# Hybrid SSD and attention layer on one core: the two parts of q and of k in one DRAM tile and one load per head pair

## The chip, the cores and the metric

The kernel runs on one core of one Trainium2 chip. The metric is the device time of one execution in microseconds (us). Three timed runs of the kernel before gave 1282.12, 1282.40 and 1283.06 us, a median of 1282.4 us. One further execution was recorded by the hardware profiler; all rows quoted in this document are of such recorded executions.

## The reference

One decoder layer over 1024 tokens of width 1024, all in float32. A normalised input goes through one wide projection, whose columns feed two branches; the branches are gated, merged, projected once more and added to the input:

```
h    = rmsnorm(x, pre_g)
proj = h @ w_in              # -> z_ssm, xBC, dt, q, k, v, f, z_att, g_ssm, g_att
y    = ssd(silu(conv(xBC)), dt, ...)  -> * silu(z_ssm) -> group rmsnorm     # Mamba-2 branch
F    = cumsum(log_sigmoid(f + fgate_b))
for each block of 128 queries, 16 heads of 64:
    s = (q . k) / 8 + F[query] - F[key], causal
    o = softmax(s) @ v
y_att  = o * silu(z_att)
merged = sigmoid(g_ssm) * (y @ w_branch_ssm) + sigmoid(g_att) * (y_att @ w_branch_att)
x + rmsnorm(merged @ w_out, post_g)
```

What the change touches is `q . k`: the scores of the attention branch.

## The kernel before, in words

**Arithmetic.** A float32 product is made from matmuls with rounded operands ("fp32r"): each operand is split into a rounded high part and the rest, the low part, and a product is the sum of three matmuls: high by high, high by low, low by high. The large matrix products (projection, branches, output) run on blocks of 512 with a scheme of seven block products in place of eight. The classes and helpers for it make a stream of steps: a weight block `raw` (256 KB) is loaded from DRAM (L344, SyncE's queue), sums of blocks are formed by VectorE (L357), ScalarE rounds the high part (L351), VectorE takes the rest (L352), TensorE multiplies into PSUM banks `pb`, `pc`, `pd` (recorded at L130, where every matmul has its line), and ScalarE and VectorE empty the banks into `s` (L404) and `th`, `u` (L412 to L418). The operands named `x0h`, `x0l` to `x6h`, `x6l` are the high and low parts of the input blocks; they are loaded (L265) and split (L280, L281) ahead of their step.

**Stages.** Until about 660 us the kernel computes the projection and, woven into it, the Mamba-2 branch. From about 665 to 1120 us it runs attention, head pair by head pair, while the stream of block products goes on beside it (first the remaining projections, `za`, the gates `gs` and `ga`, then the branch products). From 1120 us to the end come the merge, the output projection and the last norm.

**q and k.** After their projection, q and k come out transposed: channels on the 128 partitions (two heads of 64 make one head pair, of which there are 8, `NK`), tokens along the row. `parts` (L642) handles each half of the tokens (`ch`): ScalarE writes the scaled, rounded high part into a tile `hi` (L652), VectorE the rest in place (L653), and the two are stored to two DRAM tiles, the high one through ScalarE's DMA queue (L654) and the low one through SyncE's queue SP (L655). The DRAM tiles are `qh_dram`, `ql_dram`, `kh_dram`, `kl_dram`, each [8 head pairs, 128 partitions, 1024 tokens].

**Attention.** A head pair has six groups of query blocks:

```
GROUPS = [((7, 6), 1), ((7, 6), 0), ((5, 4), 1), ((5, 4), 0), ((3, 2), 0), ((1, 0), 0)]
```

The first entry is a pair of query blocks, the second is the half of the keys. For these groups the loads are issued ahead, by `loads(m)` (L1587): `load_q` (L1322) brings 256 query columns of the high and of the low part into one tile `q` [128, 2, 256], which has two buffers, with two DMAs of 128 KB, `load_k` (L1329) brings 512 key columns of both parts into one tile `k` [128, 2, 512], with one buffer for each half of the keys, with two DMAs of 256 KB, and then the forget-gate bias `fb` [128, 2, 512], broadcast to all partitions, with a third of 512 KB (L1335). `scores` makes three pairs of matmuls from q and k into the bank `s`, VectorE adds the bias and takes the row extreme `nm` (L1474), ScalarE takes the exponential `ex` (L1478), TensorE transposes it (`pt`, L133, the line of every transpose), and ScalarE or VectorE copy it out as `p` (L1515, L1517) for the product with v (`av`).

**What sets the order.** The Python code of attention yields after each piece of work, and an interleaver gives the stream of block products its turns beside it, so the order in which instructions stand in each engine's queue comes from modelled costs and from the order of the program. Each engine then works through its own queue strictly in order, and waits on semaphores. SP issues nearly all loads (x, `raw`, q, k, `fb`, x0 to x6, `y`) and some stores (`za_dram`, the low parts); ScalarE issues stores too, among them the gates `gs_dram` and `ga_dram` (L622) and the high parts (L654). The tiles `th` come from one pool with four buffers.

Of the kernel before, what the change touches and what calls it, by code (L numbers as in the profile page):

```python
# [8 lines left out]
F32 = mybir.dt.float32  # L9
# [7 lines left out]
P = 128  # L17
T = 1024
D = 1024
NK = D // P  # L20
# [66 lines left out]
def hybrid_layer(ctx: ExitStack, tc, a, out):  # L87

    nc = tc.nc
# [25 lines left out]
    za_dram = tc.dram_tile([NK, P, T], F32, name="za_dram")  # L115
    gs_dram = tc.dram_tile([NK, P, T], F32, name="gs_dram")
    ga_dram = tc.dram_tile([NK, P, T], F32, name="ga_dram")
    qh_dram = tc.dram_tile([NK, P, T], F32, name="qh_dram")
    ql_dram = tc.dram_tile([NK, P, T], F32, name="ql_dram")
    kh_dram = tc.dram_tile([NK, P, T], F32, name="kh_dram")  # L120
    kl_dram = tc.dram_tile([NK, P, T], F32, name="kl_dram")
    v_dram = tc.dram_tile([NK, P, NT, P], F32, name="v_dram")
    ys_dram = tc.dram_tile([NK, P, T], F32, name="ys_dram")
    ya_dram = tc.dram_tile([NK, P, T], F32, name="ya_dram")
# [13 lines left out]
    def small(name="th"):  # L138
        return gp.tile([P, HALF], F32, tag="th", name=name)
# [21 lines left out]
    class Operands:  # L161
# [127 lines left out]
        def put(self, j, **parts):  # L289
            for name, raw in parts.items():  # L290
                self.made.add((name, j))
                name = "-" + name if name in ("t2", "b22") else name
                self.at[name, j] = self.step
                self.split(name, j, raw)
# [161 lines left out]
    class Stream:  # L456
# [73 lines left out]
        def half(self):  # L530
            if self.run is None:
                if self.at == len(self.steps):
                    return False
                p, which = self.steps[self.at]
                if which == 7 and p.ops is ops_a and "merged" not in fin:
                    return False
                if p.ops is ops_a and not all(p.ops.ready(OPERAND[which].strip("-"), j) for j in range(KH)):
                    return False
                self.ahead(False)
                for ops in self.building:  # L540
                    ops.some(OPERAND[which])
                self.run = p.do(which)
                next(self.run)
            else:
                for _ in self.run:
                    pass
                self.run = None
                p, which = self.steps[self.at]
                if p in self.following:
                    ops = self.following[p]  # L550
                    if ops not in self.building:
                        self.building.append(ops)
                    ops.open(OPERAND[which])
                self.ahead(True)
                self.at += 1
            for ops in self.building:
                if self.held is None:
                    ops.some()
                else:
                    self.held.append(ops)  # L560
            for chores in (self.chores, self.line):
                if chores:
                    chore = chores.pop(0)
                    if chore:
                        chore()
            self.count += 1
            for w in self.waiting:
                w[0] -= 1
            for w in [w for w in self.waiting if w[0] <= 0]:
                self.waiting.remove(w)  # L570
                w[1]()
            return True
# [53 lines left out]
    def silu_gate(dram, i):  # L626

        t = {}

        def dst(ch):  # L630
            t[ch] = small()
            return t[ch]

        def post(ch):
            th = small()
            nc.scalar.activation(th, t[ch], AF.Tanh, scale=0.5)
            nc.vector.scalar_tensor_tensor(th, th, 1.0, t[ch], ALU.add, ALU.mult)
            nc.sync.dma_start(dram[i, :, half(ch)], th)

        return dst, post  # L640

    def parts(hdram, ldram, i, scale):  # L642

        t = {}

        def dst(ch):
            t[ch] = small()
            return t[ch]

        def post(ch):  # L650
            hi = small()
            nc.scalar.activation(hi.bitcast(F32R), t[ch], AF.Copy, scale=scale)  # L652
            nc.vector.scalar_tensor_tensor(t[ch].bitcast(F32R), t[ch], scale, hi, ALU.mult, ALU.subtract)  # L653
            nc.scalar.dma_start(hdram[i, :, half(ch)], hi)  # L654
            nc.sync.dma_start(ldram[i, :, half(ch)], t[ch])  # L655

        return dst, post

# [91 lines left out]
    def conv(g, name, tile_idx):  # L750

        st = {"have": set()}

        def dst(ch):
            if "u" not in st:
                st["u"] = sp.tile([P, T + 4], F32, tag="u", bufs=2, name="u")
                nc.vector.memset(st["u"][:, 0:3], 0.0)
            return st["u"][:, 3 + ch * HALF : 3 + (ch + 1) * HALF]

        def chunk(ch):  # L760
            if name not in groups[g]:
                tag = name[0:2] if name[0] == "x" else name
                groups[g][name] = sp.tile([P, T], F32, tag=tag, bufs=2 if name[0] == "x" else 1, name=name)
            d = groups[g][name][:, half(ch)]
            u, o = st["u"], ch * HALF
            nc.scalar.activation(
                d, u[:, o + 3 : o + 3 + HALF], AF.Identity, scale=cw[:, tile_idx, 3:4],
                bias=cb[:, tile_idx : tile_idx + 1],
            )
            for j in (2, 1, 0):  # L770
                nc.vector.scalar_tensor_tensor(
                    d, u[:, o + j : o + j + HALF], cw[:, tile_idx, j : j + 1], d, ALU.mult, ALU.add
                )
            stream.after(2, lambda: silu(d, u[:, o : o + HALF]))

        def silu(d, th):

            pin(nc.scalar.activation(th, d, AF.Tanh))
            nc.vector.scalar_tensor_tensor(d, th, 1.0, d, ALU.add, ALU.mult)

        def post(ch):
            st["have"].add(ch)
            if ch == 0:
                chunk(0)
            if len(st["have"]) == 2:
                chunk(1)

        return dst, post
# [234 lines left out]
    def both(kind, i, handler):  # L1023
        return Pair(((kind, 2 * i), (kind, 2 * i + 1)), (handler(2 * i), handler(2 * i + 1)))

    def groups_pairs(g):
        return [
            both("z", g, lambda i: silu_gate(zg_dram, i)),
            Pair((("b", g), ("c", g)), (conv(g, "bt", 8 + g), conv(g, "ct", 12 + g))),
            both("q", g, lambda i: parts(qh_dram, ql_dram, i, -0.125)),  # L1030
            Pair((("x", 2 * g), ("x", 2 * g + 1)), tuple(conv(g, f"xs{j}", 2 * g + j) for j in range(2))),
            both("k", g, lambda i: parts(kh_dram, kl_dram, i, 1.0)),
            both("v", g, values),
        ]

    by_group = [groups_pairs(g) for g in range(NG)]
    order = [p for ps in by_group for p in ps]

# [96 lines left out]
    with tc.tile_pool(name="pro", bufs=1, reuse_waits="tile", side="right") as pro, tc.tile_pool(  # L1135
        name="prop", bufs=1, space=PSUM, reuse_waits="tile", side="right"
# [114 lines left out]
    with tc.tile_pool(name="ssm", bufs=1, reuse_waits="tile", side="right") as sp, tc.tile_pool(  # L1251
        name="ssmp", bufs=1, space=PSUM, reuse_waits="tile", side="right"
# [42 lines left out]
    with tc.tile_pool(name="att", bufs=1, reuse_waits="tile", side="right") as ap, tc.tile_pool(  # L1295
        name="attp", bufs=1, space=PSUM, reuse_waits="tile", side="right"
# [23 lines left out]
        q, k, v, fb = {}, {}, {}, {}  # L1320

        def load_q(hp, pair):  # L1322

            t = ap.tile([P, 2, 256], F32R, tag="q", bufs=2, name="q")
            for n, dram in enumerate((qh_dram, ql_dram)):
                nc.sync.dma_start(t[:, n, :].bitcast(F32), dram[hp, :, pair[1] * P : pair[1] * P + 256])
            q[hp, pair] = t

        def load_k(hp, h):  # L1329

            t = k[hp, h] = ap.tile([P, 2, HALF], F32R, tag=f"k{h}", name="k")
            for n, dram in enumerate((kh_dram, kl_dram)):
                nc.sync.dma_start(t[:, n, :].bitcast(F32), dram[hp, :, half(h)])
            f = fb[hp, h] = ap.tile([P, 2, HALF], F32, tag=f"fb{h}", name="fb")
            nc.sync.dma_start(f, f_dram[2 * hp : 2 * hp + 2, half(h)].unsqueeze(0).to_broadcast([P, 2, HALF]))  # L1335

# [250 lines left out]
        def loads(m):  # L1587
# [10 lines left out]
            if g == 1:  # L1598
                load_q(hp, (3, 2))
            if g == 2 and more:  # L1600
                load_k(hp + 1, 1)
# [7 lines left out]
            if g == 4 and more:  # L1609
                load_q(hp + 1, (7, 6))  # L1610
# [6 lines left out]
            if g == 5 and more:  # L1617
                load_k(hp + 1, 0)
                load_q(hp + 1, (5, 4))
# [6 lines left out]

        load_q(0, (7, 6))
        load_k(0, 1)
        load_k(0, 0)
        load_q(0, (5, 4))  # L1630
# [23 lines left out]
        for m in range(6 * NK + 1):  # L1654

            if m < 6 * NK:
                hp, g = divmod(m, 6)
# [104 lines left out]
```

## Time and profile before

| | |
|---|---|
| timed runs, median | 1282.4 us (1282.12 to 1283.06) |
| profiled execution, time | 1286.04 us |
| its span from first to last instruction | 1284.3 us |
| mean TensorE clock granted in it | 0.997 of full speed |
| DRAM traffic | 162.99 MB read, 72.34 MB written |
| largest DMA queue | 137408 packets, 197.14 MB, 48.0% of the engines' time |

How to read the rows. PE is TensorE (PEld: its weight loads), DVE VectorE, ACT ScalarE, POOL GpSimd, SP SyncE, which computes nothing and issues DMAs; SPq and ACTq are the DMA-issuing instructions of SP and ACT. A row of the timeline begins with the start in us from the span's start and the busy time in us, then engine, line of the source, operation, `out<-in` by the names in the program, shape, and a count; in brackets stands the idle time of that engine just before it and the instruction that ended the wait. A row of waits has the waiting instruction, the one that released it, then the total us, the number of waits and the longest. A row of DMA issues by line has lowest, median and highest duration of the issuing instruction in ns.

### The profile page before, as it was taken

How to read it: one execution, taken by the hardware profiler on the slowest of the kernel's cores; microseconds unless marked ns; L12 is line 12 of the kernel's file. 1: busy time of each engine (PE TensorE's matmuls, PEld its weight loads, DVE VectorE, ACT ScalarE, POOL GpSimd, SP SyncE). 2: the span in 40 equal slices, each digit the busy share in tenths (PEclk: the TensorE clock that was granted, in tenths of full speed). 3: DMA queues.
4: the chain of work that ended last, by engine and by line, in shares of the span. 5: the costliest groups of instructions: out<-in, count | busy, mean ns of one | idle time of the engine just before them, and what ended most of it. 6: DMA issues, size and time to landing. Idle time of an engine off the chain costs nothing.

```text
span 1284.3 us, 20839 instructions
## 1 busy us (share of the span) xinstructions
PE 1248.8 (97%) x6926; PEld 982.4 (76%) x6926; DVE 1015.3 (79%) x1994; ACT 793.6 (62%) x1738; POOL 311.5 (24%) x314
## 2 busy tenths in 40 slices
PE   5999999999999999999999999999999999999997
PEld 3688878787888888888877777777767777778886
DVE  7988886987888978997767677767789766886976
ACT  7745665556664765566546666666677666753754
POOL 4000440013300241114102123322111212356052
PEclk9999999999999999999999999999999999999999
DMA  8232552646436543654356566675787657765932
GB/s 298 70 116 77 152 157 86 193 148 181 133 110 205 178 134 100 221 162 134 132 170 232 173 221 202 211 233 201 238 293 243 205 180 237 248 227 195 365 112 101
DMA packets 153516, 233.57 MB, mean 182 GB/s; under 512 B 15968, under 2 KB 61504, under 8 KB 153408
## 3 DMA queue, kind: packets, MB, share of 16 engines
q1 hardware_dynamic: 137408, 197.14, 48.0%
q10 hardware_dynamic: 11136, 19.11, 3.9%
q0 software_dynamic: 4864, 15.99, 3.2%
q8 instruction: 54, 0.88, 0.3%
q14 instruction: 54, 0.44, 0.1%
HBM read 162.99 MB, written 72.34 MB: 183 GB/s over the span
## 4 chain that ended last, share of the span: by engine, by line
PE 67%; DVE 11%; DMA 9%; issue 6%; ACT 5%; POOL 1%; SPq 1%; ACTq 0%; DVEq 0%; POOLq 0%
PE pb L130 29%; PE pc L130 16%; PE pd L130 6%; PE av L130 4%; PE pt L133 4%; PE s L130 3%; DVE wop L352 2%; PE yps L130 2%; DMA raw<-in_wu 1%; ACT ex L1478 1%; DVE sum L357 1%; DMA xt<-in_x 1%; ACT wop L351 1%; DMA rb<-st_dram 1%; PE tr_v L133 1%
## 5 line engine op out<-in xcount | busy, mean ns | idle before, releaser
L352 DVE TENSOR_TENSOR wop<-sum,wop 128x512 fp32r<-128x512 f32 x180 | 140.9, 784 | 53.6 <-ACT wop L351 52.4
L351 ACT ACTIVATE wop<-sum 128x512 fp32r<-128x512 f32 x180 | 112.4, 626 | 109.4 <-DVE sum L357 52.8
L1478 ACT ACTIVATE ex<-ex,nm 128x512 f32<-128x512 f32 (+1 forms) x192 | 116.2, 606 | 76.4 <-DVE nm L1474 74.4
L404 ACT ACTIVATE s<-pb 128x512 f32<-128x512 f32 x144 | 85.1, 591 | 92.1 <-PE pb L130 88.9
L130 PE MATMUL pc<-x3h,wop 128*128 128x512 f32 x384 | 129.8, 396 | 2.7 <-DVE th L414 2.3
L130 PE MATMUL pc<-x2h,wop 128*128 128x512 f32 x384 | 131.3, 400 | 1.0 <-DVE u L416 1.0
L130 PE MATMUL pb<-x0h,wop 128*128 128x512 f32 x384 | 130.8, 397 | 0.0
L130 PE MATMUL pb<-x6h,wop 128*128 128x512 f32 x384 | 129.5, 395 | 1.3 <-ACT s L404 1.3
L130 PE MATMUL pb<-x5h,wop 128*128 128x512 f32 x384 | 130.1, 396 | 0.7 <-ACT s L404 0.7
L130 PE MATMUL pb<-x4h,wop 128*128 128x512 f32 x384 | 129.2, 395 | 0.0
L352 DVE TENSOR_TENSOR wop<-raw,wop 128x512 fp32r<-128x512 f32 x144 | 106.2, 739 | 26.8 <-ACT wop L351 26.5
L1474 DVE CUSTOM_DVE_ANT_0 ex<-s,fb 128x512 f32<-128x512 f32 (+1 forms) x192 | 97.1, 552 | 20.9 <-PE s L130 15.2
L351 ACT ACTIVATE wop<-raw 128x512 fp32r<-128x512 f32 x144 | 89.6, 623 | 12.3 <-PE pd L130 5.9
L130 PE MATMUL pd<-x1h,wop 128*128 128x512 f32 x288 | 96.3, 394 | 0.0
L130 PEld LDWEIGHTS pc<-x3h,wop 128*128 128x128 f32 x384 | 72.1, 188 | 19.9 <-DVE th L414 2.7
L130 PEld LDWEIGHTS pc<-x2h,wop 128*128 128x128 f32 x384 | 72.6, 189 | 18.8 <-issue 2.4
L130 PEld LDWEIGHTS pb<-x6h,wop 128*128 128x128 f32 x384 | 72.1, 188 | 18.6 <-issue 2.0
L130 PEld LDWEIGHTS pb<-x5h,wop 128*128 128x128 f32 x384 | 72.1, 188 | 18.5 <-issue 2.0
L130 PEld LDWEIGHTS pb<-x0h,wop 128*128 128x128 f32 x384 | 72.1, 188 | 17.4 <-issue 2.9
L130 PEld LDWEIGHTS pb<-x4h,wop 128*128 128x128 f32 x384 | 72.1, 188 | 16.8 <-issue 1.9
L213 POOL TENSOR_TENSOR wd<-wd 128x256 f32<-128x256 f32 x32 | 33.7, 1052 | 206.3 <-DMA wd<-in_wo 119.7
L133 PE MATMUL pt<-ident,ex 128*128 128x128 f32 x576 | 76.7, 276 | 4.4 <-DVE nm L1474 2.4
(311 smaller groups left out, 2986.4 us busy)
## 6 DMA issues: line engine op xcount, KB each, us to landing
raw<-in_wu SPq DMA_DIRECT2D x128, 256.0 KB
csb<-cs_dram SPq DMA_DIRECT2D x32, 256.0 KB
fb<-f_dram SPq DMA_DIRECT2D x16, 512.0 KB
rb<-st_dram SPq DMA_DIRECT2D x48, 128.0 KB
wd<-in_wo SPq DMA_DIRECT2D x40, 128.0 KB
xt<-in_x SPq DMA_DIRECT2D x8, 512.0 KB
gs_dram<-th ACTq DMA_DIRECT2D x16, 256.0 KB
qh_dram<-th ACTq DMA_DIRECT2D x16, 256.0 KB
```

The costliest lines, as they stand in the source:

```text
L130: return tc.keep_in_program_order(nc.tensor.matmul(*args, **kw))
L133: return tc.keep_in_program_order(nc.tensor.transpose(out_, in_, idn))
L213: pin(nc.gpsimd.tensor_tensor(t[out_], t[a_], t[b_], ALU.subtract))
L351: nc.scalar.activation(op[:, 0], src, AF.Copy)
L352: nc.vector.tensor_tensor(op[:, 1], src, op[:, 0], ALU.subtract)
L357: self.adds.tensor_tensor(t, x, y, ALU.add)
L404: nc.scalar.activation(s, ps, AF.Copy)
L1474: nc.vector.tensor_tensor_reduce(o, s[e][:, 0:w], fb[hp, h][:, e, 0:w], 1.0, 3.0e38, ALU.add, ALU.min, nm)
L1478: pin(nc.scalar.activation(o, o, AF.Exp, scale=-1.0, bias=nm, accum_out=hd.at(hd.sm, i, h, e)))
```

## The change

The two parts of q lie in one DRAM tile, and so do the two of k: [8 head pairs, 2 parts, 128 partitions, 1024 tokens]. `parts` stores the high part to index 0 and the low part to index 1; sizes, queues and order of the stores are as they were. `load_q` and `load_k` issue one DMA in place of two: its source is the DRAM tile with its part and partition dimensions exchanged, so that a partition receives two pieces, 256 (q) or 512 (k) floats from each part, into the same SBUF tile as before. The matmuls, their operands and the tiles in SBUF are unchanged. The line numbers of the kernel after are lower by 2 from the DRAM tiles on, and by 3 behind `load_q` and `load_k`.

```
-    qh_dram = tc.dram_tile([NK, P, T], F32, name="qh_dram")
-    ql_dram = tc.dram_tile([NK, P, T], F32, name="ql_dram")
-    kh_dram = tc.dram_tile([NK, P, T], F32, name="kh_dram")
-    kl_dram = tc.dram_tile([NK, P, T], F32, name="kl_dram")
+    q_dram = tc.dram_tile([NK, 2, P, T], F32, name="q_dram")
+    k_dram = tc.dram_tile([NK, 2, P, T], F32, name="k_dram")
...
-    def parts(hdram, ldram, i, scale):
+    def parts(dram, i, scale):
...
-            nc.scalar.dma_start(hdram[i, :, half(ch)], hi)
-            nc.sync.dma_start(ldram[i, :, half(ch)], t[ch])
+            nc.scalar.dma_start(dram[i, 0, :, half(ch)], hi)
+            nc.sync.dma_start(dram[i, 1, :, half(ch)], t[ch])
...
-            both("q", g, lambda i: parts(qh_dram, ql_dram, i, -0.125)),
+            both("q", g, lambda i: parts(q_dram, i, -0.125)),
...
-            both("k", g, lambda i: parts(kh_dram, kl_dram, i, 1.0)),
+            both("k", g, lambda i: parts(k_dram, i, 1.0)),
...
             t = ap.tile([P, 2, 256], F32R, tag="q", bufs=2, name="q")
-            for n, dram in enumerate((qh_dram, ql_dram)):
-                nc.sync.dma_start(t[:, n, :].bitcast(F32), dram[hp, :, pair[1] * P : pair[1] * P + 256])
+            cols = slice(pair[1] * P, pair[1] * P + 256)
+            nc.sync.dma_start(t.bitcast(F32), q_dram[hp, :, :, cols].rearrange("n p c -> p n c"))
...
             t = k[hp, h] = ap.tile([P, 2, HALF], F32R, tag=f"k{h}", name="k")
-            for n, dram in enumerate((kh_dram, kl_dram)):
-                nc.sync.dma_start(t[:, n, :].bitcast(F32), dram[hp, :, half(h)])
+            nc.sync.dma_start(t.bitcast(F32), k_dram[hp, :, :, half(h)].rearrange("n p c -> p n c"))
```

## The prediction

> **What bounds the kernel now.** I read the page's first lines, then busy time by stretch, then what TensorE (PE) waited for while attention runs (660 to 1125 us), then the rows around its gaps.
>
> ```profile
> span 1284.3 us, 20839 instructions
> PE 1248.8 (97%) x6926; PEld 982.4 (76%) x6926; DVE 1015.3 (79%) x1994; ACT 793.6 (62%) x1738; POOL 311.5 (24%) x314
> ...
> 665.00:690.00 25.00, 22.68 (x108) 17.94 (x107) 17.66 (x32) 9.98 (x18) 2.60 (x4) 1.00 0.86 296
> 690.00:945.00 255.00, 254.45 (x1728) 193.31 (x1728) 183.77 (x494) 169.73 (x430) 66.78 (x84) 1.00 0.65 213
> 945.00:970.00 25.00, 21.96 (x116) 15.63 (x116) 19.83 (x43) 17.73 (x44) 3.49 (x5) 0.86 0.78 271
> ```
>
> The last three rows are stretches: length, then busy PE, weight loads, DVE, ACT, POOL, then granted clock, DMA share, GB/s. PE is the bound. From 690 to 945 it is idle for 0.55 of 255 us; a transfer that only comes earlier there is worth nothing. In two stretches of 25 us it loses 2.3 and 3.0 us, and in the second its clock is 0.86 on average. Those two are all that this change can reach.
>
> ```profile
> PE pt L133 <- DVE nm L1474: 2.4, 3, 1.3
> PE pc L130 <- DVE th L414: 2.3, 1, 2.3
> PE s L130 <- DVE p L1515: 1.7, 3, 0.9
> PE pt L133 <- ACT ex L1478: 1.6, 1, 1.6
> PE s L130 <- ACT p L1517: 0.3, 2, 0.2
> PE pc L130 <- DVE x3l L281: 0.3, 1, 0.3
> ```
>
> These are all the waits of PE from 660 to 1125 us (total us, times, longest). No DMA is among them: no matmul of the scores ever waited for q or k. The reason is how early the loads go out; the shortest leads I found are these:
>
> ```profile
> 769.86 0.42 SPq L1326 DMA_DIRECT2D q<-ql_dram  x1
> ...
> 782.07 0.51 PE L130 MATMUL s<-k,q 64*128 64x256 f32 x4
> ...
> 836.58 0.42 SPq L1333 DMA_DIRECT2D k<-kl_dram  x1
> ...
> 849.80 0.50 PE L130 MATMUL s<-k,q 64*128 64x512 f32 x2
> ```
>
> 12.2 us for q and 13.2 us for k, from issue to first use.
>
> **The change, part by part.** *Removed:* one request in two, 32 of q and 16 of k.
>
> ```profile
> L1326 SPq DMA_DIRECT2D q<-ql_dram x32: 319/428/948, 666.2 to 1101.8; - x32
> ```
>
> At a median of 0.43 us that is some 48 x 0.43 = 21 us of SP's time. SP computes nothing and PE never waits for what it loads here, so this counts 0; if that cover were gone, it would be 0.43 us per load. Bytes, pieces in DRAM (1 KB and 2 KB) and stores stay the same. The instruction listings of the two programs agree on every engine up to the first q load at 665.7 us, so nothing before it moves. PE's matmuls lose one DMA wait inside each group of scores that starts a new q or k; as no such wait shows above, 0.
>
> *Moved:* PE, ACT and POOL keep their order to the instruction. DVE moves one `L357` behind two others, and SP's requests, once pairs are counted as one, change places in five spots. Two consequences can be priced.
>
> **A, at 670 to 677 us.**
>
> ```profile
> 666.76 0.38 SPq L1333 DMA_DIRECT2D k<-kh_dram  x1
> 667.23 0.38 SPq L638 DMA_DIRECT2D za_dram<-th  x1
> 667.66 0.94 SPq L344 DMA_DIRECT2D raw<-in_wu  x2
> 668.65 0.48 SPq L1333 DMA_DIRECT2D k<-kl_dram  x1
> 669.19 0.42 SPq L1335 DMA_DIRECT2D fb<-f_dram  x1
> ...
> 675.02 0.69 DVE L357 TENSOR_TENSOR sum<-raw 128x512 f32<-128x512 f32 x1 [3.59 <-DMA raw<-in_wu]
> 675.63 0.68 DVE L414 TENSOR_TENSOR th<-pc,s 128x512 f32<-128x512 f32 x1
> 676.23 0.68 DVE L352 TENSOR_TENSOR wop<-raw,wop 128x512 fp32r<-128x512 f32 x1
> ...
> 676.37 0.50 PE L130 MATMUL pc<-x3h,wop 128*128 128x512 f32 x1 [2.32 <-DVE th L414]
> ...
> 681.07 0.68 DVE L352 TENSOR_TENSOR wop<-sum,wop 128x512 fp32r<-128x512 f32 x1
> 684.66 0.39 PE L130 MATMUL pc<-x2h,wop 128*128 128x512 f32 x1
> ...
> 958.30:965.10 6.80, 6.02 (x19) 4.24 (x19) 6.38 (x13) 6.17 (x16) 2.82 (x4) 0.50 1.00 373
> ```
>
> DVE stands 3.59 us at `L357` for weights (`raw`) still under way. Behind it in DVE's queue is `L414`, which empties PE's bank `pc`; so PE waits 2.32 us. In the changed program `L414` and its follower `L352` come ahead of `L357`: DVE is free at 671.4, and PE can go on without the gap. Gain 2.3.
>
> Part comes back. SP now issues the whole k and fb ahead of `raw`: the low half of k (256 KB) and fb (512 KB), 768 KB more. The last row shows what the DMA engines move when full, 373 GB/s; 786 kB take 2.1 us. `raw` then lands at about 677.1. `L414` and `L352`, 0.6 us each, are done by then, so what follows `L357` runs 2.1 - 1.2 = 0.9 us later than now. The tightest follower is the operand of `pc<-x2h`: ready at 681.07 + 0.68, with 0.9 more 682.7. PE, 2.3 us earlier, wants it at 682.3. It loses 0.3 to 0.4; A is worth **2.0**. Bounds: 2.3 if `raw` lands in time; 0 or a little below if it lands 3 us later still.
>
> **B, at 947 to 965 us.** The compiled program gives the requests of SP and ACT eight completion semaphores in turn, so each waits until the eighth one before it has landed.
>
> ```profile
> 947.46 0.43 SPq L1333 DMA_DIRECT2D k<-kl_dram  x1
> 947.99 1.52 SPq L1335 DMA_DIRECT2D fb<-f_dram  x1
> 949.56 0.47 SPq L1326 DMA_DIRECT2D q<-qh_dram  x1
> 950.07 0.43 SPq L1326 DMA_DIRECT2D q<-ql_dram  x1
> 950.54 1.85 SPq L265 DMA_DIRECT2D x3l<-t_s  x4
> 952.50 0.37 SPq L1538 DMA_DIRECT2D y<-ya_dram  x1
> ...
> 953.35 0.33 ACTq L622 DMA_DIRECT2D ga_dram<-th  x1
> 953.72 1.15 ACT L280 ACTIVATE x1h<-x1l 128x512 fp32r<-128x512 f32 x2 [4.09 <-DMA fb<-f_dram]
> ...
> 957.67 0.44 PE L133 MATMUL pt<-ident,ex 128*128 128x128 f32 x2 [1.61 <-ACT ex L1478]
> 958.97 0.48 PE L133 MATMUL pt<-ident,ex 128*128 128x128 f32 x1 [0.86 <-DVE nm L1474]
> ```
>
> Counting back from ACT's store `ga_dram<-th`: y, four x3l, two q, fb. fb is the eighth. ACT's queue is in order, so it stood 4.09 us until fb landed, although nothing in ACT needs fb. Queued behind the store are the split of x1 and then the exponentials, and PE's transposes waited for these, 1.61 + 0.86 = 2.47 us. With the pairs merged the eighth before is k: y, four x3l, q, fb, k. k lies in front of fb in the queue; fb's 524 kB take 1.4 us at 373 GB/s, so k lands about 1.4 us earlier, and one request less lets SP be up to 0.43 us earlier. I take 1.6 (1.4 to 1.8) off ACT's stand, and it passes one to one to PE: the first gap closes (957.67 - 1.6 = 956.1, when PE had finished), the second stays. B is worth **1.6**. Bounds: 0 if k lands no sooner than fb did; 2.47 if both gaps close.
>
> **Sum.** 2.0 + 1.6 = 3.6 us. There is a third term in the profiled execution: right after B's gaps the granted clock is 0.50 for 6.8 us (row quoted under A), which costs about 6.8 x 0.5 = 3.4 us. The profiled execution took 1286.04 us (1284.3 of span, 1.7 around it), 3.6 above the median of 1282.4. The 3.4 is nearly that whole difference, so I take it that the timed runs mostly go without the slow clock. Profiled: 1286.04 - 3.6 - 3.4 = 1279.0. Timed, and my forecast: 1282.4 - 3.6 = **1278.8**.
>
> **The rivals.**
> *1. The slow clock is in the timed runs too.* For it: the gaps behind it are in the program, not in the profiler. Against: the gap of 2.32 us at 676 shows no drop, and the timed runs lie within 1 us. Then 1282.4 - 3.6 - 3.4 = 1275.4. [...]
>
> *2. Given back.* PE reaches later waits 3.6 us earlier, and these are set by transfers: `raw` behind 768 KB more, stores that hold a buffer of `th`. With A at 0 and B at 0 to 1.6: 1280.8 to 1282.4. For it: the DMA engines are at 0.86 of their time from 665 to 690. Against: they have room after (0.65).
>
> [...]
>
> *4. The change does not do what it says:* excluded, the listing of SP has 48 requests fewer.
>
> **How the numbers follow.** Faster or slower means by more than 0.2% (2.6 us), about what a measurement of this kernel can tell from no change. Forecast 0.38 (1277.5 to 1281; 0.26 of it below 1279.8); rival 1, 0.24, all faster; rival 2, 0.22, of which 0.05 still faster; rival 3 and its milder forms 0.16, slower. Faster 0.55, same 0.29, slower 0.16. The range leaves out most of rival 3 and the lowest end of rival 1 (A and B at their upper bounds with the clock): 1274 to 1285; the forecast's own is 1277.5 to 1281.
>
> **What would show it.** A: PE's wait `pc <- DVE th L414` of 2.3 us is gone, and DVE's wait for `raw` stands behind `L414`. B: ACT's wait at `x1h` shrinks from 4.1 to about 2.5 us with k as its releaser, PE's two gaps sum to about 0.9, and no stretch near 960 has a clock of 0.50. Rival 2: new waits of DVE on `raw` or `th` between 676 and 692. [...] I am wrong if the order on SP brings a new stand of ACT elsewhere, or if PE's idle time after 665 us is what it is now.

## The result, and the profile after

| | before | after |
|---|---|---|
| timed runs beside each other, 12 of each, median | 1283.79 us | 1279.31 us |
| their range | 1282.12 to 1285.89 | 1277.12 to 1283.03 |
| ratio | | 0.9968 (95% interval 0.9961 to 0.9976) |
| profiled execution: time, span | 1286.04, 1284.3 us | 1278.67, 1277.0 us |

The changed kernel is 4.1 us faster (0.0032 x 1283.8; 3.1 to 5.0). Forecast were 3.6 us less and a time of 1278.8 us, counted from the 1282.4 us of three runs; the twelve of the table have 1283.8. The total and the two places are right; how large each term is, and what the clock does in the timed runs, is not, as the runs below show.

First the page of the kernel after, its span and engines:

```profile
span 1277.0 us, 20793 instructions
PE 1246.0 (98%) x6926; PEld 980.9 (77%) x6926; DVE 1009.9 (79%) x1994; ACT 795.1 (62%) x1738; POOL 312.4 (24%) x314
```

46 recorded instructions fewer, the same work, and PE is still the bound. Then the same three stretches, with the same columns as those of before:

```profile
665.00:690.00 25.00, 24.53 (x121) 19.57 (x119) 19.24 (x40) 12.06 (x24) 2.64 (x5) 1.00 0.92 322
690.00:945.00 255.00, 254.48 (x1730) 193.70 (x1729) 181.19 (x491) 170.93 (x435) 66.22 (x84) 1.00 0.63 211
945.00:970.00 25.00, 22.71 (x147) 16.79 (x147) 23.30 (x55) 20.45 (x47) 4.05 (x6) 1.00 0.89 312
```

In the first PE's idle time went from 2.3 to 0.5 us; in the long middle it was 0.55 and is 0.52; in the third it went from 3.0 to only 2.3, but the clock is 1.00 where it was 0.86. All waits of PE from 660 to 1125 us, after:

```profile
PE pt L131 <- DVE nm L1471: 1.8, 3, 0.9
PE pt L131 <- ACT ex L1475: 1.5, 3, 0.9
PE s L128 <- DVE p L1512: 0.9, 1, 0.9
PE pb L128 <- ACT s L402: 0.7, 1, 0.7
PE pc L128 <- DVE th L416: 0.5, 1, 0.5
```

The wait of 2.3 us for `th` of the line that was L414 (now L412) is gone; again no DMA stands here. At place A, the timelines of VectorE and PE of the kernel after:

```profile
671.04 0.69 DVE L412 TENSOR_TENSOR th<-pc,s 128x512 f32<-128x512 f32 x1
671.71 0.69 DVE L350 TENSOR_TENSOR wop<-raw,wop 128x512 fp32r<-128x512 f32 x1
674.60 0.69 DVE L355 TENSOR_TENSOR sum<-raw 128x512 f32<-128x512 f32 x1 [2.21 <-DMA raw<-in_wu]
```

```profile
673.56 0.39 PE L128 MATMUL pc<-x3h,wop 128*128 128x512 f32 x1
```

VectorE still stands 2.21 us for `raw`, but behind L412, and PE's `pc<-x3h`, which now has no bracket, waits for nothing. At place B, the requests of SP, the queue of ScalarE and PE's gaps:

```profile
943.11 0.53 SPq L1330 DMA_DIRECT2D k<-k_dram  x1
943.75 0.40 SPq L1332 DMA_DIRECT2D fb<-f_dram  x1
944.21 0.46 SPq L1324 DMA_DIRECT2D q<-q_dram  x1
944.76 2.60 SPq L263 DMA_DIRECT2D x3l<-t_s  x4
947.46 0.44 SPq L1535 DMA_DIRECT2D y<-ya_dram  x1
```

```profile
948.26 0.33 ACTq L620 DMA_DIRECT2D ga_dram<-th  x1
948.64 1.15 ACT L278 ACTIVATE x1h<-x1l 128x512 fp32r<-128x512 f32 x2 [2.79 <-DMA fb<-f_dram]
```

```profile
952.59 0.44 PE L131 MATMUL pt<-ident,ex 128*128 128x128 f32 x2 [0.40 <-ACT ex L1475]
953.89 1.24 PE L131 MATMUL pt<-ident,ex 128*128 128x128 f32 x6 [0.86 <-DVE nm L1471]
956.23 0.77 PE L131 MATMUL pt<-ident,ex 128*128 128x128 f32 x5 [0.88 <-ACT ex L1475]
```

Counted back from the store, y, four x3l, q, fb and k: the eighth is k, and ACT stands 2.79 us where it stood 4.09. The profile puts the wait down to fb, the load that landed nearest to its end; but the store carries the same completion semaphore as k here (109 in the trace; fb has 100), and in all ten traces in which ACT issues it, the same as the eighth request before it. PE's first gap has shrunk from 1.61 to 0.40 us, the second is as it was, and a third one of 0.88 us is new.

The order of PE's 6926 matmuls is the same in both programs, so the start of the same matmul can be compared. By how much the execution after is ahead at each, in us:

```
matmul of before at     668.35   676.37   951.40   957.67   964.57  1083.58     last
ahead by                  0.32     2.81     3.86     5.08     6.58     7.23     7.32
```

A is the step of 2.5 us at 676. B is the step of 1.2 us at 957, and 1.5 us more while the clock of before is at half. 1.05 us come in smaller steps between 676 and 951 and 0.65 us up to 1083, which were not forecast. Nor is all of A's step a gain: the programs are the same up to 665.7 us, yet the execution after was ahead by 1.30 us at 660 and had lost all but 0.32 of it by 668. The two profiled executions lie 7.3 us apart, the timed ones 4.1: one trace is one draw, so the sizes have to come from more than one.

### The profile page after: what moved, and what is told of

The parts are those of the page before. It is cut to its first block, busy times and chain, and to the rows that moved or that the text cites. A ratio compares the mean times of both kernels' runs of the same rounds, so it can differ in the third digit from the quotient of the medians.

```text
span 1277.0 us, 20793 instructions
## 1 busy us (share of the span) xinstructions
PE 1246.0 (98%) x6926; PEld 980.9 (77%) x6926; DVE 1009.9 (79%) x1994; ACT 795.1 (62%) x1738; POOL 312.4 (24%) x314
## 4 chain that ended last, share of the span: by engine, by line
PE 75%; DVE 8%; DMA 6%; ACT 5%; issue 4%; POOL 1%; SPq 1%; DVEq 0%; ACTq 0%; POOLq 0%
PE pb L128 31%; PE pc L128 18%; PE pd L128 6%; PE av L128 4%; PE pt L131 4%; PE s L128 4%; PE yps L128 2%; DVE wop L350 1%; ACT ex L1475 1%; PE st L128 1%; DMA xt<-in_x 1%; DMA th<-ys_dram 1%; DVE ex L1471 1%; PE tr L131 1%; PE tr_v L131 1%
## 5 line engine op out<-in xcount | busy, mean ns | idle before, releaser
L350 DVE TENSOR_TENSOR wop<-sum,wop 128x512 fp32r<-128x512 f32 x180 | 137.8, 767 | 52.0 <-ACT wop L349 51.0
L128 PEld LDWEIGHTS pb<-x0h,wop 128*128 128x128 f32 x384 | 72.1, 188 | 17.4 <-issue 2.9
```

The lines of the kernel that those rows point to most:

```text
L128: return tc.keep_in_program_order(nc.tensor.matmul(*args, **kw))
L350: nc.vector.tensor_tensor(op[:, 1], src, op[:, 0], ALU.subtract)
```

## The experiments

Since the matmuls, ACT and POOL keep their order, the terms can be set apart by merging only some of the loads. The theories: **1**, the gain is the order on VectorE at A and the eighth request at B; **2**, it comes from there being fewer requests; **3**, it comes from the new place of the parts in DRAM.

**Both loads, new DRAM tiles** (two_loads, and once more as two_loads_2):

```
-            nc.sync.dma_start(t.bitcast(F32), q_dram[hp, :, :, cols].rearrange("n p c -> p n c"))
+            for n in range(2):
+                nc.sync.dma_start(t[:, n, :].bitcast(F32), q_dram[hp, n, :, cols])
```

and k likewise.

> The DRAM tiles are those of the changed kernel, but every pair is still loaded in two requests; the order on all engines is that of the kernel before. Theory 1 (the gain comes from two places where the order and the semaphore turn changed, A at 676 us and B at 953 us): 0, ratio 1.000, PE's wait of about 2.3 us at 676 and ACT's stand of about 4 us at 953 are there. Theory 2 (fewer requests as such, 4.1 us for 48): 0. Theory 3 (the layout in DRAM, high beside low): the whole gain, ratio 0.997.

> The new DRAM tiles with two loads each, once more, since the first time gave 0.9987 (0.9976 to 0.9999) where theory 1 has 1.000 and theory 3 (layout) 0.997. If the layout is worth something, 0.998 to 0.999 again; if it was scatter, 1.000 within 0.001.

Measured: 0.9987 (0.9976 to 0.9999) and 0.9990 (0.9979 to 1.0002), some 1.5 us less than before, twice. The waits that theory 1 names are there. ACT's queue and PE's waits of the first:

```profile
948.66 1.15 ACT L278 ACTIVATE x1h<-x1l 128x512 fp32r<-128x512 f32 x2 [4.43 <-DMA fb<-f_dram]
```

```profile
PE pt L131 <- ACT ex L1477: 2.5, 2, 2.1
PE pt L131 <- DVE nm L1473: 2.2, 3, 1.1
...
PE pc L128 <- DVE th L412: 0.5, 1, 0.5
```

But the wait at A is 0.5 us and not 2.3, in a program whose order is that of before. The whole gain is not in the layout; that some 1.5 us may be, at the edge of what can be measured, stays open.

**Only head pair 0 merged** (first_pair): `if hp == 0:` one load, else two.

> Only the requests of head pair 0 are merged, 6 fewer of 48. Theory 1: A alone, since VectorE's L355 moves behind L412 and at 953 us fb is still the eighth request before the gate store: -2.3 to -2.5 us, ratio about 0.998; the wait of PE at 676 is gone, ACT stands about 4 us at 953 and PE's gaps there sum to about 2.5. Theory 2: 6/48 of 4.1 us, -0.5 us, ratio 0.9996.

Measured: 0.9993 (0.9985 to 1.0002). VectorE's order is the new one, and the wait at A is gone; ACT still stands 4.31 us for fb. All waits of PE from 660 to 1125 us:

```profile
PE pt L131 <- ACT ex L1483: 1.9, 1, 1.9
PE pt L131 <- DVE nm L1479: 1.8, 3, 0.8
PE s L128 <- DVE p L1520: 0.9, 1, 0.9
PE pc L128 <- DVE x3l L279: 0.3, 1, 0.3
PE av L128 <- ACT p L1522: 0.2, 1, 0.2
PE s L128 <- ACT p L1522: 0.2, 1, 0.2
```

The wait went as expected, but the time fell by 0.9 us and not by 2.3 to 2.5, and against two_loads, from which it was to differ in A alone, by nothing that can be told (medians 1282.39 and 1282.65 us on the same chip).

**All but head pair 0** (other_pairs): the condition turned round.

> All requests but those of head pair 0 are merged, 42 fewer of 48. Theory 1: B alone: -1.2 us, and up to -2.7 where the slow clock behind it also goes, ratio 0.998 to 0.999; PE's wait of 2.3 us at 676 stays. Theory 2: 42/48 of 4.1 us, -3.6 us, ratio 0.9972.

Measured: 0.998 (0.9964 to 0.9996), within theory 1. ACT's stand is 3.21 us:

```profile
951.75 1.16 ACT L278 ACTIVATE x1h<-x1l 128x512 fp32r<-128x512 f32 x2 [3.21 <-DMA fb<-f_dram]
```

PE's wait at A, for L412, is 0.2 us here, although VectorE has the old order: the 2.3 us do not come every time.

**Only k** (k_only) and **only q** (q_only) merged:

> Only k is merged, 16 requests fewer; VectorE's order is that of before and fb is the eighth request before the gate store at 953 us. Theory 1: neither A nor B, 0 us, ratio 0.9995 to 1.0005, both waits as before. Theory 2: 16/48 of 4.1 us, -1.4 us, ratio 0.999.

> Only q is merged, 32 requests fewer. VectorE's order is that of before; at 953 us the eighth request before the gate store is the low half of k in place of fb. Theory 1: B alone, -1.2 to -2.7 us, ratio 0.998 to 0.999, with PE's 2.3 us at 676 still there. Theory 2: 32/48 of 4.1 us, -2.7 us, ratio 0.9979 (not told apart by the time alone; by the waits).

Measured: k alone 0.9999 (0.9988 to 1.0009), q alone 0.9985 (0.9975 to 0.9996). That is theory 1: with k alone, fb is still the eighth request and nothing is gained; with q alone it is k's low half. The stand of each, first k alone, then q alone:

```profile
951.35 1.16 ACT L278 ACTIVATE x1h<-x1l 128x512 fp32r<-128x512 f32 x2 [3.27 <-DMA fb<-f_dram]
```

```profile
948.98 1.15 ACT L278 ACTIVATE x1h<-x1l 128x512 fp32r<-128x512 f32 x2 [2.82 <-DMA k<-k_dram]
```

For theory 2, 16 requests fewer give nothing that can be measured, and its 1.4 us are at the edge of k's interval. Its 2.7 and 3.6 us for q_only and other_pairs lie within theirs too, so by time alone it is made unlikely, not excluded. But it names no wait, and none for q or k stands in any of these traces.

**The stands taken away with nothing merged.** In the kernel before, the one gate store at B is issued by POOL (before_pool), the one sum at A is formed by POOL (before_sum), or both (before_both):

```
-            self.adds.tensor_tensor(t, x, y, ALU.add)
+            (nc.gpsimd if self.keys[0] == ("gs", 2) and x is self.raw.get("a21") else self.adds).tensor_tensor(t, x, y, ALU.add)
...
-            nc.scalar.dma_start(dram[i, :, half(ch)], t[ch])
+            (nc.gpsimd if dram is ga_dram and (i, ch) == (7, 1) else nc.scalar).dma_start(dram[i, :, half(ch)], t[ch])
```

> The kernel before, with nothing merged, but the one gate store ga_dram at 953 us is issued by POOL in place of ACT, so that ACT has no semaphore turn to wait for there. If ACT's stand for fb is what makes PE's gaps at 957 us, as theory 1 has it: ACT's wait of 4.1 us at x1h is gone, PE's gaps of 1.62 and 0.86 us shrink to 0.9 or less in all, no half clock near 960: -1.6 to -4 us, ratio 0.997 to 0.9988. If the gaps come from elsewhere (theory 2): they stay, 0 us, ratio 1.000.

> The kernel before, nothing merged, but the one sum of raw at which VectorE stands near 675 us is formed by POOL. A alone. The six traces with VectorE's old order so far show PE waits there of 2.3, 0.5, 0.8, 0.5, 0.2 and 1.2 us (mean 0.9), the four with the new order none. Theory 1: no wait of PE at pc behind L414, 0.9 us less, ratio 0.999 to 1.000. Theory 2 (fewer requests): 0.

> The kernel before, nothing merged, with both stands taken away in another way: the sum of raw near 675 us on POOL, the gate store at 953 us issued by POOL. Theory 1 (the two stands are the whole gain): at least the gain of the change, -3 to -5 us, ratio 0.996 to 0.998. Theory 2 (fewer requests) and theory 3 (layout): 0 from the request count and layout, ratio 1.000. That the store alone gave 0.9997 (0.9985 to 1.0009) speaks for something like 0.999.

Measured: 0.9997 (0.9985 to 1.0009), 1.0008 (0.9999 to 1.0016) and 0.9989 (0.9980 to 0.9997). The named waits do go: ACT does not stand at B in before_pool and before_both, and PE does not wait for L414 at A in before_sum and before_both. The split of x1 in before_pool, without a bracket:

```profile
945.90 1.14 ACT L280 ACTIVATE x1h<-x1l 128x512 fp32r<-128x512 f32 x2
```

But the time follows only in part. For before_both, two stretches and PE's waits from 660 to 1125 us show why:

```profile
945.00:975.00 30.00, 28.54 (x183) 21.06 (x182) 27.60 (x68) 23.73 (x57) 4.59 (x7) 1.00 0.88 287
975.00:990.00 15.00, 12.40 (x56) 8.52 (x55) 11.53 (x27) 9.84 (x25) 1.07 (x2) 0.77 0.78 263
```

```profile
PE pt L133 <- ACT ex L1478: 1.8, 3, 0.9
PE s L130 <- ACT p L1517: 1.6, 2, 1.5
PE s L130 <- DVE p L1515: 1.4, 2, 1.1
```

B's stretch runs at full clock now, and the next one does not: PE arrives earlier at matmuls of the scores (`s`), waits there 1.5 and 1.1 us for the copies `p` of ACT and VectorE, and the clock falls to half 0.8 us behind the first of these (0.77 on average over the 15 us). The stand was the bound of its place; behind it lay another. The sum on POOL has a price too: from the matmul at 640.2 us to that at 946.3 (times of before) before_sum and before_both took 305.0 us each, the seven kernels with VectorE's old order 304.5 on average (303.4 to 306.1), the five in which merging moved the sum 303.2 (302.5 to 304.1). So before_sum and before_both are no clean measure of A.

**The changed kernel with that store on POOL** (after_pool, after_pool_2), beside the changed kernel again (after_again):

> The changed kernel with the same one store on POOL. Theory 1: ACT's remaining wait of 2.8 us goes; PE's gaps near 953 to 957 us sum to 2.1 us in the changed kernel, of which 1.3 (0.40 and 0.88, both behind ACT) can go: 1 us less than the changed kernel, ratio to before about 0.996.

> The changed kernel with the one gate store on POOL, once more, since the first ratio of 0.9957 rests on five runs: 0.9957 if the remaining stand of ACT costs PE about 1 us, 0.9968 if it costs nothing.

> The changed kernel again, as the measure for the others on the same chip: ratio 0.9961 to 0.9976 to the kernel before.

Measured: 0.9957 (0.9945 to 0.9969) and 0.9965 (0.9952 to 0.9978), against 0.9969 (0.9958 to 0.9980) for the changed kernel. If it is better, it is by less than can be told. The second trace of it shows the same give-back as before_both:

```profile
975.00:990.00 15.00, 12.05 (x56) 8.40 (x54) 11.84 (x29) 8.36 (x19) 2.25 (x4) 0.77 0.55 182
```

**All traces side by side.** For each: PE's wait at A, the eighth request before the gate store and ACT's stand behind it, the length of half clock between 950 and 990 us, and the time between the same two matmuls (the 5150th and the 5290th, 946.3 and 975.1 in before), then on to the 5900th (1066.9). "new" is VectorE's order with L357 behind L414, "sum" the sum on POOL. All in us, worked out from the starts in the traces.

```
kernel        order  wait A  eighth  stand  half clock   B stage  next stage
before        old      2.3    fb      4.1      6.8        28.79     91.86
two_loads     old      0.5    fb      4.4      3.4        27.75     91.75
two_loads_2   old      0.7    fb      4.5      6.8        28.39     91.75
k_only        old      0.8    fb      3.3      -          26.16     91.78
before_sum    sum      0      fb      4.4      6.8        28.42     91.72
first_pair    new      0      fb      4.3      6.8        28.33     91.74
q_only        old      0.5    k       2.8      3.4        26.82     92.32
other_pairs   old      0.2    k       3.2      3.4        27.25     91.72
after         new      0      k       2.8      -          25.44     91.98
after_again   new      0      k       1.3      -          24.17     92.45
before_pool   old      1.2    none    -        -          24.19     92.91
before_both   sum      0      none    -        6.8        24.71     96.52
after_pool    new      0      none    -        -          24.16     92.76
after_pool_2  new      0      none    -        6.8        24.29     96.92
```

The wait at A: seven times the old order, 0.9 us on average and 0.2 to 2.3; seven times another one, 0. ACT's stand: 4.2 on average with fb as the eighth, 2.5 with k. The B stage: 28.0 with fb, 25.9 with k, 24.3 with the store on POOL; of the 3.6 us that POOL gains on fb, the next stage gives 2.9 back (94.8 on average, against 91.9 for the others). The kernels with k give back too: their next stage takes 92.1, that of those with fb 91.8. Over both stages k gains 1.7 us on fb, and the groups overlap: k_only, with fb, has a shorter B stage than q_only and other_pairs.

## Why the prediction was right, and where it was not

- **Removed requests, 0:** right as far as the waits show. q's 64 requests are 32 and k's 32 are 16, and issuing one takes about as long as a single part took (median 0.39 us for q, 0.38 and 0.43 for its two parts before; 0.38 for k, 0.35 and 0.46 before). The lines of q and of k, after:

```profile
L1324 SPq DMA_DIRECT2D q<-q_dram x32: 360/390/974, 665.4 to 1092.6; - x32
```

```profile
L1330 SPq DMA_DIRECT2D k<-k_dram x16: 370/383/596, 666.0 to 1054.1; - x16
```

No wait of PE names a DMA after 660 us, before or after, so the saved time is not on the path.

- **A, 2.0 us:** the mechanism is right, the size is not. The wait of 2.32 us from which it was worked out is the longest of seven; their mean is 0.9. `raw` lands now sooner, now later behind the same requests, and a term that hangs on one landing can't be read from one trace.

  Counted from the start of the matmul at 668.35 in before, VectorE's sum of `raw` starts 6.7 us later in before, 5.6 in before_pool and 4.6 to 5.2 in the other five with the old order, and PE's wait is in all seven what goes beyond 4.3 us, to within 0.1. That `raw` lands later behind k and fb is right: with the new order the sum starts 6.6 us after that matmul on average, 1.3 later than with the old (5.2); 2.1 were forecast. But the 0.3 us that were to come back did not: no such trace has a wait of PE at `pc<-x2h` behind A.

  From 668.35 to 687.8 us (times of before) the seven old-order traces took 17.4 to 19.5 us (mean 18.0), the seven others 16.8 to 16.9, so A is worth 1.2 us there, without overlap. At 946 the kernels with the new order by merging are 1.3 us ahead on average (304.5 against 303.2 above), but there the ranges overlap. In the timed runs A alone shows nothing: first_pair is no faster than two_loads. Whether A's gain reaches the end is therefore not shown.

- **B, 1.6 us:** ACT's stand fell by 1.65 us (4.18 to 2.53 on average), as worked out from fb's and k's landing. That the turn of the semaphores sets it is shown from four sides: it is long in every kernel where fb is the eighth, short where k is, with q alone and not with k alone, and gone where ACT does not issue the store. The two groups nearly touch, though (3.3 in k_only, 3.2 in other_pairs), and the mean rests on six and four traces. PE's first gap shrank by 1.2 and a third one of 0.88 us, behind `ex`, came into view: that it is missing in the trace of before because PE, at half clock, arrived too late to wait is likely, not shown.

  So the stand's 1.6 us did not pass one to one to PE, and the gaps sum to 2.1 us where 0.9 were forecast. With the clock the stage is 2.1 us shorter, and 1.7 with the one behind it: near the forecast 1.6, but in good part by way of the clock, which the prediction had left out of the timed runs; that its size fits is luck.

- **The slow clock, taken to be only in the profiled execution:** wrong. This step ("the timed runs mostly go without the slow clock") rested on the profiled time lying 3.6 us above a median of three. That execution has a mean clock of 0.997 with the drop in it; the timed runs have no more. Over 91 timed runs the kernel before took 1280.8 to 1289.5 us with a mean granted clock of 0.9964; 21 runs of the changed kernel had 0.9974. Within the kernels a run is 0.8 us longer for each 0.001 of clock less (229 runs, correlation -0.55), so some 0.8 us of the gain go with the clock: rival 1 was a part of the answer. That is a correlation, and the mean clock also counts the last 1.6 to 4.8 us, which run at half in every trace.

  Rival 1's price was too high for this place: 6.8 us at half were priced at 3.4, but cost 1.5 in the comparison of the matmuls, in which the kernel after waits 0.88 us instead. Between kernels with the same three gaps, 3.4 us at half cost 1.1 (other_pairs against k_only) and 1.4 (q_only against after), priced at 1.7. In the next stage 6.8 us at half went with 3.6 and 4.2 us more (before_both against before_pool, after_pool_2 against after_pool), longer waits for copies included. The drops ahead of the kernel's last 5 us all last 3.4 or 6.8 us, and of two kernels with the same three gaps (k_only with 0.79, 0.87 and 0.88 us, other_pairs with 0.81, 0.86 and 0.88) the second has the drop and the first has not (a granted clock of 0.94 and of 1.00 on average from 945 to 975 us). What decides between the two is not shown.

- **Rival 2, given back:** its sign did not come: VectorE has no wait for a load of `raw` or for a store that holds a `th` between 676 and 692 us in the kernel after; its longest wait there is 2.0 us, for ACT's `wop`, and the kernel before has one of 2.1. A stand of ACT of 1.4 us for a load did come up elsewhere (at 769.08, before a copy `p`) and one of 1.7 us at 714.19 went; PE waits for nothing at the new one. Giving back as such did happen, most of all with the store on POOL (2.9 of 3.6 us), where it is a copy `p` by ACT that comes late, not a transfer: PE waits for it 1.5 us in before_both, 1.8 in after_pool_2, 0.5 and 0.6 in before_pool and after_pool, 0 and 0.3 in after and after_again.

- **Rival 3, a merged request that takes longer than its two parts:** did not happen; none of the fourteen traces has a wait of PE for q or k. The median landing of the merged loads, after:

```profile
q<-q_dram SPq DMA_DIRECT2D x32, 256.0 KB, 4.2
k<-k_dram SPq DMA_DIRECT2D x16, 512.0 KB, 6.7
```

These medians rest on the few landings that the trace tells, four of q (2.7 to 4.9 us) and three of k (5.9 to 6.8). They lie far inside leads of 12 to 13 us. That a merged request could be slow enough for PE to wait was the author's guess, and no run shows one.

- **The sum:** 3.6 forecast, 4.1 (3.1 to 5.0) measured. The traces give 1.2 for A and 1.7 for B with its clock and the stage behind it, 2.9 us. The prediction put the layout at 0, but two_loads, which has nothing else, came out some 1.5 us faster than before, twice; by these ratios the change gains some 2.6 us on it, about A and B.

  The layout's share is not explained. With the old order PE's wait at A is 2.3 and 1.2 us with the old tiles and 0.2 to 0.8 with the new, but in before_sum and before_both, with the old tiles, `raw` landed as early as with the new (POOL's sum starts 5.2 and 4.6 us after the matmul at 668.35), so the tiles are not shown to set it. The single parts do not add up in the timed runs: each has an interval of 1 to 2 us either way, as wide as the terms. That 3.6 lies so near to 4.1 is therefore partly luck: A was taken too large, and the clock in the timed runs and the layout were left out. That the change is faster, and that both stands shorten as told, is shown; the shares of A, B and the layout in the 4.1 us stay open.

## What to carry to other kernels

The change to the number of DMAs moved two things here that no line of it names: the order that the scheduler gives the engines behind the loads (PE's wait at A is 0.9 us on average with the old one and 0 with the new), and which earlier transfer a later DMA has to wait for, since this program gives out its completion semaphores in turn (ACT's stand is 4.2 us on average with fb as the eighth request, 2.5 with k). Look for an instruction that stands for a transfer that it does not use, count back to it, and put a transfer there that lands early. Take the size of such a wait from several traces, since one shows one draw (0.2 to 2.3 us for the wait at A), and ask what is late next: the store on POOL took the stand away and gave most of it, 2.9 of 3.6 us, back from 20 us later on.

## What the hardware showed besides

The clock fell to half without a gap of PE over 2.4 us at B: in five of the six traces with fb as the eighth request PE had a gap of 1.6 to 2.4 us at B, and the drop began between 0.1 us before its end and 2.1 us behind it (in before at 958.3, behind the gap that ended at 957.67). In other_pairs, with k as the eighth request, no gap there was over 0.88 us, and the clock fell all the same.

A load of the same size behind the same requests did not land at the same time: with the order of before, VectorE's stand for `raw` at A was 3.6 us in before, 2.5 in before_pool, whose edit comes only at 953 us, and 1.8 us in two_loads.
